# Six reorderings in a two-layer attention and retention block: the modulation tiles in halves, keys and decays, output weights' room, the feed-forward middle block, the first retention head's queries, the second feed-forward's first weights

## The chip, the cores and the metric

The kernel runs on one core of one Trainium2 chip. The metric is the device time of one execution in microseconds (us), from the runs of the kernel; a profile of one execution shows what each engine did. Engines are named as the profile names them: PE (TensorE matmuls), PEld (TensorE weight loads), DVE (VectorE), ACT (ScalarE), POOL (GpSimd), SP (the queue that issues most transfers).

## What is computed

Two layers work on 512 latent tokens and 256 context tokens of width 1024. Layer 0 mixes tokens by windowed grouped-query attention, layer 1 by retention that runs in both directions; each is followed by a SwiGLU feed-forward. All of it is modulated by shifts, scales and gates made from a condition vector ("ada").

```python
for i in range(2):
    mx = split(silu(c) @ ada_w[i] + ada_b[i], 6)          # latent: shift, scale, gate, twice
    mc = split(silu(c_ctx) @ ada_w[i] + ada_b[i], 6)      # context
    h_x = rms_norm(x, norm1_g[i]) * (1 + mx[1]) + mx[0]
    h_c = rms_norm(y_ctx, norm1_g[i]) * (1 + mc[1]) + mc[0]
    if i == 0:    # 16 query heads, 4 key/value heads of 64, q and k normed, 2-D rotary on the latent side,
                  # window of 128 to each side plus all context keys, a sink logit per head
        out_c, out_x = windowed_gqa_sink(h_x, h_c, ...)
    else:         # 4 heads, 256 wide in q and k, 512 wide in v; log decays = log_sigmoid(decay_logit)
        out_c, out_x = bidir_retention(h_x, h_c, ...)     # out = (silu(gate) * norm(o)) @ w_o
    x = x + mx[2] * out_x
    x = x + mx[5] * swiglu(rms_norm(x, norm2_g[i]) * (1 + mx[4]) + mx[3], ffn_w_in[i], ffn_w_out[i])
    # layer 0 does the same for y_ctx with mc
```

The data are fp32.

## The kernel before, in words

**Products.** Matrices are kept transposed, width on the 128 partitions and tokens along the free axis. A float32 product is made of three fp32r matmuls on split operands: a raw weight tile `wraw` (128x1024, one transfer of 512 KB) is cast on ACT to `whi`, and DVE subtracts to get `wlo` (`split`, L165/L166; `next_w`, L140/L141; `split_chunk`, L1321/L1322); activations are split the same way. `mm3` (L148 to L150), `product` (L997), `product_q` (L1391) and `product_v` (L1404) issue hi x hi, hi x lo, lo x hi. Many blocks use a Strassen-like scheme on quarters of a matrix ("seven", seven products instead of eight), with sums of quarters formed on DVE.

**Stages**, by the profile's time: a prologue (0 to 76 us) with the sums of squares, the modulation columns ("ada quarters") and keys and values; queries and attention (76 to 315); the output projection (to about 365); the first feed-forward (to about 860) for latent and context; retention, four heads one after the other (to about 1390); the second feed-forward.

**Order.** Up to the first values of the context a block under `tc.manual_schedule` keeps PE, DVE and ACT in the order in which the code is written. After it a scheduler of the framework orders the instructions of each engine; `after(ins, others)` adds an edge, and the rooms (a tile of a pool is free when its last reader is done) add others. `steps[n]` is a table of functions to be called at step n of attention.

**What the change touches.**

- `ada_quarter_load`, `quarter_product` (L335), `quarter_columns` (L343, L344), `first_quarter` (L353, L357) and `ada_quarter` (L373, L377): quarter q of the modulation is 32 small matmuls on four tiles `adan`, a copy of the resulting rows (ACT, 128x256), two transposes on PE, and some small DVE operations that give the columns. In quarter 0 the scale half is done first; in quarters 1 to 3 both halves go together.
- `hidden0` (L465, L468, L472) makes the modulated hidden tiles `h`, hi and lo, for two of the eight width tiles k; `keys(s, q)` (L481) and `values(s, q)` (L495) use them, s = 0 for latent, 1 for context.
- `rope_key`, `key_factor`, `key_parts` and the loop ahead of them norm, rotate and split the keys; the block `dec` to `dcol` makes the decays of layer 1 from 8 numbers per partition.
- `next_w(wo_p)` takes the four raw tiles of the attention's output weights, `wsel` chooses the room of a raw tile; `w01` is the first feed-forward weight, which waits for `scaled`.
- `seven` of the first feed-forward (L1130 to L1157), 20 times, and `last_sum` (L318, L1058, L1079), which makes the last sums of tokens.
- In a retention head the queries `qt` get their last sums at L1546 and L1549, `rope_pair` rotates them (L1413 to L1415), and sums of the gate and value weights are made at L1564, L1565 and L1571, then split at L1321/L1322 for `product_v`.
- `seven` of the second feed-forward (L1827 on), whose weights b32 and b14 are split at L165/L166.

## Time and profile before

| | |
|---|---|
| runs | 1735.02 us median of 3 (1733.53 to 1737.07) |
| the profiled execution | 1735.58 us, its span 1733.8 us |
| mean granted TensorE clock | 0.999 |
| PE busy | 1705.7 us, 98% of the span, 11092 matmuls |
| DVE busy | 1331.9 us, 77% |
| ACT busy | 843.9 us, 49% |
| DMA | 205.67 MB, mean 119 GB/s |

The span runs from the first to the last instruction that the profile shows; the execution's own time is 1.8 us longer. Matmuls are pipelined, so one that lasts 0.39 us in the table is followed by the next after 0.23 us, and a gap of PE is read from the bracket behind a row: the idle time just before it, and what ended it. Times in the stages are counted from the span's start.

### The profile page before, as it was taken

To read this page: it belongs to the slowest core of one execution; us is meant where nothing else is said; L and a number is where in the kernel's file an instruction comes from. 1 tells how busy PE (TensorE), PEld (TensorE's weight loads), DVE (VectorE), ACT (ScalarE), POOL (GpSimd) and SP (SyncE) were. 2 spreads that over 40 slices of the span, in tenths; PEclk is the share of its full clock that TensorE was granted. 3 is DMA by queue.
4 is the path that set the end of the run, shared out by engine and by line. 5 is a ranking of instruction groups with operands and counts; after the bars stand their busy time and mean duration, and the time that the engine had idled before them with its cause. 6 is when DMAs were issued, how large, how long until landed. Compare 5 with 4: busy or idle time off the path is not lost.

```text
span 1733.8 us, 28152 instructions
## 1 busy us (share of the span) xinstructions
PE 1705.7 (98%) x11092; PEld 1536.9 (89%) x11092; DVE 1331.9 (77%) x2370; ACT 843.9 (49%) x1506; POOL 121.9 (7%) x266
## 2 busy tenths in 40 slices
PE   7999999999999999999999999999999999999999
PEld 5878887899999999999998888898898999999998
DVE  5887796388778787877898858758768898778774
ACT  5667786264434343342564634524525555445442
POOL 0033443000000000000000000000000100000000
PEclk9999999999999999999999999999999999999999
DMA  9510015142234434343423533433433223233322
GB/s 374 201 50 25 14 47 174 49 146 98 98 134 135 138 120 155 110 146 115 141 99 122 176 103 126 158 110 124 158 107 112 98 98 122 74 122 100 107 75 85
DMA packets 61908, 205.67 MB, mean 119 GB/s; under 512 B 6864, under 2 KB 7760, under 8 KB 61648
## 3 DMA queue, kind: packets, MB, share of 16 engines
q1 hardware_dynamic: 54864, 178.71, 29.9%
q0 software_dynamic: 6912, 25.17, 4.4%
q8 instruction: 87, 1.43, 0.3%
q14 instruction: 45, 0.37, 0.1%
HBM read 201.75 MB, written 2.10 MB: 118 GB/s over the span
## 4 chain that ended last, share of the span: by engine, by line
PE 88%; DVE 6%; ACT 3%; DMA 2%; issue 1%; POOL 0%; SPq 0%; DVEq 0%; ACTq 0%
PE Y L997 15%; PE Z L1404 8%; PE Z L997 7%; PE pj L148 6%; PE pj L150 6%; PE pj L149 6%; PE Y L1391 3%; PE X L997 3%; PE pj L1404 3%; PE pO L813 2%; PE pT L788 2%; PE S L768 2%; PE X L1391 2%; PE Z L150 1%; PE Z L149 1%; PE Z L148 1%
## 5 line engine op out<-in xcount | busy, mean ns | idle before, releaser
L165 ACT CAST whi<-wraw 128x1024 fp32r<-128x1024 f32 x98 | 102.4, 1051 | 185.1 <-PE Z L150 75.1
L997 PE MATMUL Y<-aq,whi 128*128 128x384 f32 x640 | 173.7, 335 | 2.4 <-ACT whi L165 1.3
L254 DVE SCALAR_TENSOR_TENSOR res<-pj,mod,res 128x512 f32<-128x512 f32 (+1 forms) x102 | 74.4, 730 | 76.7 <-PE pj L150 75.7
L166 DVE TENSOR_TENSOR wlo<-wraw,whi 128x1024 fp32r<-128x1024 f32 x98 | 119.4, 1223 | 8.9 <-ACT whi L165 8.5
L997 PEld LDWEIGHTS Y<-aq,whi 128*128 128x128 f32 x640 | 116.5, 188 | 3.8 <-ACT hn L1145 1.6
L140 ACT CAST whi<-wraw 128x1024 fp32r<-128x1024 f32 x75 | 78.5, 1048 | 74.5 <-PE Z L150 25.6
L141 DVE TENSOR_TENSOR wlo<-wraw,whi 128x1024 fp32r<-128x1024 f32 x75 | 91.5, 1221 | 25.3 <-ACT whi L140 24.7
L997 PE MATMUL Y<-aq,wlo 128*128 128x384 f32 x320 | 107.0, 334 | 0.0
L272 DVE CUSTOM_DVE_ANT_0 y<-adaw,crow,small_sb 128x1024 bf16<-128x1024 f32 x64 | 81.9, 1279 | 29.3 <-DMA adaw<-in_adaT_dram 29.2
L1321 ACT CAST whi<-wraw 128x1024 fp32r<-128x1024 f32 x55 | 57.6, 1050 | 71.8 <-PE Y L150 52.6
L1404 PE MATMUL Z<-whi,sA 128*128 128x512 f32 x256 | 81.7, 395 | 3.0 <-ACT whi L1321 3.0
L101 ACT ACTIVATE pr<-pr,stat,qs 128x513 f32<-128x513 f32 (+2 forms) x96 | 74.0, 774 | 16.9 <-DVE stat L775 15.1
L1322 DVE TENSOR_TENSOR wlo<-wraw,whi 128x1024 fp32r<-128x1024 f32 x55 | 66.9, 1222 | 17.1 <-ACT whi L1321 17.0
L782 POOL TENSOR_SCALAR pr<-pr,stat 128x512 f32<-128x512 f32 (+2 forms) x96 | 65.1, 693 | 84.5 <-DVE stat L779 78.1
L148 PE MATMUL pj<-ax,whi 128*128 128x512 f32 x176 | 68.9, 391 | 1.3 <-DVE res L254 1.3
L150 PE MATMUL pj<-ax,whi 128*128 128x512 f32 x176 | 68.7, 390 | 0.0
L149 PE MATMUL pj<-ax,wlo 128*128 128x512 f32 x176 | 68.5, 389 | 0.0
L269 POOL DMA_DIRECT2D adaw<-in_adaT_dram x48 | 25.6, 533 | 513.4 <-DVE mod L272 420.9
L769 DVE CUSTOM_DVE_ANT_0 pr<-S,mask,qs 128x256 f32<-128x256 f32 (+1 forms) x96 | 52.7, 567 | 10.8 <-PE S L768 7.2
L997 PE MATMUL Y<-sA,whi 128*128 128x256 f32 x304 | 60.5, 282 | 0.1
L1404 PEld LDWEIGHTS Z<-whi,sA 128*128 128x128 f32 x256 | 48.5, 190 | 13.2 <-ACT whi L1321 3.5
L997 PEld LDWEIGHTS Y<-aq,wlo 128*128 128x128 f32 x320 | 60.1, 188 | 0.0
(615 smaller groups left out, 5479.9 us busy)
## 6 DMA issues: line engine op xcount, KB each, us to landing
wraw<-in_wst_dram SPq DMA_DIRECT2D x231, 512.0 KB, 3.6
adaw<-in_adaT_dram POOLq DMA_DIRECT2D x48, 512.0 KB, 3.7
wx<-in_wst_dram SPq DMA_DIRECT2D x28, 512.0 KB, 4.4
adan<-in_adaQ_dram SPq DMA_DIRECT2D x16, 512.0 KB, 7.0
adan<-in_adaN_dram SPq DMA_DIRECT2D x16, 512.0 KB, 7.4
res<-in_xT_dram SPq DMA_DIRECT2D x16, 256.0 KB, 5.3
q<-in_adaN_dram SPq DMA_DIRECT2D x16, 256.0 KB, 3.2
aq<-in_adaN_dram SPq DMA_DIRECT2D x12, 256.0 KB, 5.3
```

Source lines behind the costliest of these rows:

```text
L140: after(nc.scalar.copy(hi, raw), behind)
L141: after(nc.vector.tensor_tensor(lo, raw, hi, op=sub), low)
L148: after(nc.tensor.matmul(o, whi, xhi, start=first, stop=False), behind)
L149: nc.tensor.matmul(o, wlo, xhi, start=False, stop=False)
L150: return nc.tensor.matmul(o, whi, xlo, start=False, stop=last)
L165: nc.scalar.copy(hi, t)
L166: return nc.vector.tensor_tensor(lo, t, hi, op=sub)
L254: return nc.vector.scalar_tensor_tensor(res[d], o, mods[l, s][:, part, d:d + 1], res[d], mult, add)
L272: after(nc.vector.tensor_tensor_reduce(junk, w, cr[:, s * 1024:(s + 1) * 1024], 1.0, sm_t[:, C_ADAB + l * 48 + j:C_ADAB + l * 48 + j + 1], ...
L997: ins = nc.tensor.matmul(o, p, r, start=first and k + i == 0, stop=k == 3 and i == 2, skip_group_check=not first)
L1391: ins = nc.tensor.matmul(o[:, e * SC:(e + 1) * SC], p[:, ws], r, start=first and k + e + i == 0, stop=k == 3 and i == 2, skip_group_check= ...
L1404: ins = nc.tensor.matmul(o, p, r, start=first and k + i == 0, stop=k == 3 and i == 2, skip_group_check=not first)
```

## The change

It alters the order and the rooms of existing work in six places; the matmuls that carry the arithmetic stay.

1. **Quarters.** `first_quarter` goes, and every quarter is done as quarter 0 was: the scale half (product, copy, transpose, columns), then the shift half. One block of values stands as fill behind each half's copy. The tiles come in the order 2, 3, 0, 1 in each quarter. The matmul that added the last square is replaced by one more DVE addition. `hidden0` issues its multiplications ahead of its ACT operations. The latent `keys` go width tile by width tile.
2. **Keys and decays.** The latent keys' norm and rotation stand earlier; the decays become a function that step 13 of attention calls, behind the scores of block 6.
3. **Output weights' room.** The four raw tiles are taken with `wsel` 2, 3, 4, 5 instead of 0, 2, 3, 1, with four parts of their own in `wo_p`; `w01` waits for nothing but its room.
4. **First feed-forward.** `last_sum` is called in the middle of the first `seven`, behind the split of b24. In every `seven` the cast of the third weight b3 stands behind the copy of the first product.
5. **First retention head.** The queries are rotated between the splits of the two third weights, no longer ahead of the gate and value weights; the rooms of `gate` change.
6. **Second feed-forward.** b14 is split ahead of b32; the casts wait for the last finished block, the subtractions for other additions of the output before.

```diff
     def ada_quarter_load(q):
-        for i in (2, 3, 0, 1) if q == 0 else range(4):
+        for i in (2, 3, 0, 1):
...
+    def ada_quarter(q, w, copy, scale_fill, shift_fill, middle=None):
         o, t = pT()[:, 0:256], pT()[:, 0:256]
+        scales, shifts = (T(st_p, P, "rows", 2) for _ in range(2))
+        quarter_product(o, w, 1)
+        copy(scales, o[:, P:])
+        scale_fill()
+        nc.tensor.transpose(t[:, P:], scales, ident)
+        quarter_columns(q, t, 0, (1,))
+        if middle:
+            middle()
+        quarter_product(o, w, 0)
         nc.scalar.copy(shifts, o[:, 0:P])
+        shift_fill()
+        nc.tensor.transpose(t[:, 0:P], shifts, ident)
+        return lambda: quarter_columns(q, t, 0, (0,)), lambda: quarter_columns(q, t, 1)
-    def ada_quarter(q, w, fill):
-        o = pT()[:, 0:256]
-        for part in range(2):
-            quarter_product(o, w, part, range(4))
-        rows = t_sq(256)
-        nc.scalar.copy(rows, o)
-        fill()
-        t = pT()[:, 0:256]
-        for part in range(2):
-            nc.tensor.transpose(t[:, part * P:(part + 1) * P], rows[:, part * P:(part + 1) * P], ident)
-        quarter_columns(q, t, 0)
-        return lambda: quarter_columns(q, t, 1)
...
     def keys(s, q):
-        steps = [(j, a, b) for j in range(2) for a, b in ((0, 0), (1, 0), (0, 1))]
+        two = (2 * q, 2 * q + 1)
         if s == 0:
-            steps = [steps[i] for i in (0, 1, 3, 4, 2, 5)]
+            steps = [(j, a, 0, k) for k in two for a in range(2) for j in range(2)]
+            steps += [(j, 0, 1, k) for k in two for j in range(2)]
...
-        values(0, 0, (0,))
-        c1 = ada_quarter(1, wq[1], lambda: values(0, 0, (1,)))
+        c0, c1 = ada_quarter(1, wq[1], nc.scalar.copy, lambda: values(0, 0, (0,)), lambda: values(0, 0, (1,)))
...
-        c1 = ada_quarter(3, wq[3], lambda: values(0, 2, (0,)))
+        c0, c1 = ada_quarter(3, wq[3], nc.scalar.copy, lambda: values(0, 2, (0,)), lambda: values(0, 2, (1,)))
+        hidden0(0, 6, 7, shifts=c0, at=1)
         c1()
-        hidden0(0, 6, 7)
-        values(0, 2, (1, 2, 3))
+        values(0, 2, (2, 3))
...
+    def decays(behind):
...
+    steps.setdefault(13, []).append(lambda: decays([blocks[6].scored]))
...
-    for wsel[0] in (0, 2, 3, 1):
-        wo.append(cut(next_w(wo_p)))
+    for wsel[0] in (2, 3, 4, 5):
+        wo.append(cut(next_w(wo_p, 4)))
...
-    def seven():
+    def seven(middle=None):
...
         half = split(g, *b24)
+        if middle:
+            middle()
         nc.vector.tensor_tensor(u[:, l_], u[:, r_], u[:, l_], op=sub)
         b3 = w_parts(fp, 1)
-        split(u, *b3)
+        third = nc.scalar.copy(b3[0], u)
+        nc.vector.tensor_tensor(b3[1], u, b3[0], op=sub)
...
         product(Y, operand["11"], b11, 0, True)
-        after(rounded[0], [nc.scalar.copy(c11, Y)])
+        ins = [nc.scalar.copy(c11, Y)]
+        after(rounded[0], ins)
+        after(third, ins)
...
-    w01 = [next_w(fp, 1, behind=[scaled])]
+    w01 = [next_w(fp, 1)]
...
-                if f == PLAIN:
-                    last_sum()
-                a, end = seven()
+                a, end = seven(last_sum if f == PLAIN else None)
...
-        qh = rope_pair(qt, cos1, sin1)
         if hd:
+            qh = rope_pair(qt, cos1, sin1)
             other_values()
...
-        w3 = [split_chunk(g) for g in g12]
+        w3 = [split_chunk(g12[0])]
+        if not hd:
+            qh = rope_pair(qt, cos1, sin1)
+        w3.append(split_chunk(g12[1]))
...
-            gate[2:4], vt[2:4] = vt[2:4], gate[2:4]
+            gate, vt[2:4] = vt[2:4] + gate[0:2], gate[2:4]
...
-        after(split(u, *b32), added[0:1])
-        after(split(g, *b14), added[1:2])
+        for (hi, lo), t, i in ((b14, g, 1), (b32, u, 2)):
+            after(nc.scalar.copy(hi, t), finished[-1:] if added else [])
+            after(nc.vector.tensor_tensor(lo, t, hi, op=sub), added[i:i + 1])
```

What the engines then do is shown at three places. The first is PE in the prologue, at quarter 1 (the 32 small matmuls `pT<-adan,ccol`, and the transposes from `const_sb`, the identity). Before:

```order
L495 MATMUL kvv<-wlo,h 128x256
L495 MATMUL kvv<-whi,h 128x256
L335 MATMUL pT<-adan,ccol 32x128 x32
L495 MATMUL kvv<-whi,h 128x256
L495 MATMUL kvv<-wlo,h 128x256
L495 MATMUL kvv<-whi,h 128x256 x2
L495 MATMUL kvv<-wlo,h 128x256
L495 MATMUL kvv<-whi,h 128x256
L377 MATMUL pT<-const_sb,sq 128x128 x2
```

Now:

```order
L335 MATMUL pT<-adan,ccol 32x128 x16
L482 MATMUL kvv<-whi,h 128x256
L482 MATMUL kvv<-wlo,h 128x256
L482 MATMUL kvv<-whi,h 128x256 x2
L482 MATMUL kvv<-wlo,h 128x256
L482 MATMUL kvv<-whi,h 128x256
L355 MATMUL pT<-const_sb,rows 128x128
L335 MATMUL pT<-adan,ccol 32x128 x16
L482 MATMUL kvv<-whi,h 128x256
L482 MATMUL kvv<-wlo,h 128x256
L482 MATMUL kvv<-whi,h 128x256 x2
...
L362 MATMUL pT<-const_sb,rows 128x128
```

The 32 small matmuls now come in two groups of 16, with a block of values and a transpose behind each; the block that stood ahead of them stands between them.

The second place is DVE at the first `seven` of the first feed-forward. `wraw<-wraw` of 128x512 are the sums of weight quarters, the row at L1133 (now L1125) the last sum that the split of b24 waits for; `crow<-act` and the `aq` behind it are the last sums of tokens. Before:

```order
L1132 TENSOR_TENSOR wraw<-wraw 128x512
L166 TENSOR_TENSOR aq<-act,aq 128x384 x8
L1058 TENSOR_TENSOR crow<-act 128x384 x3
L1079 TENSOR_TENSOR act<-hn,act 128x384
L1058 TENSOR_TENSOR crow<-act 128x384
...
L166 TENSOR_TENSOR aq<-crow,aq 128x384 x2
L1079 TENSOR_TENSOR act<-hn,act 128x384
L166 TENSOR_TENSOR aq<-crow,aq 128x384 x2
L1133 TENSOR_TENSOR wraw<-wraw 128x512
L166 TENSOR_TENSOR wlo<-wraw,whi 128x1024
```

Now:

```order
L1124 TENSOR_TENSOR wraw<-wraw 128x512
L166 TENSOR_TENSOR aq<-act,aq 128x384 x2
L1125 TENSOR_TENSOR wraw<-wraw 128x512
L166 TENSOR_TENSOR aq<-act,aq 128x384 x2
L166 TENSOR_TENSOR wlo<-wraw,whi 128x1024
L1068 TENSOR_TENSOR hn<-hn,Y 128x384
L166 TENSOR_TENSOR aq<-act,aq 128x384 x8
L1050 TENSOR_TENSOR crow<-act 128x384 x3
...
L166 TENSOR_TENSOR aq<-crow,aq 128x384 x2
L1133 TENSOR_TENSOR wlo<-wraw,whi 128x1024
```

The last weight sum and the low part behind it have moved ahead of the sums of tokens.

The third place is DVE in the first retention head. `wx<-wx` (L1565, now L1560) is the sum for the second weight of the product on values, `gate` the queries' last sums, `hn` and `sq` the rotation (L1413 to L1415, now L1408 to L1410), `wlo<-wx,whi` the low part of a split. Before:

```order
L1322 TENSOR_TENSOR wlo<-wx,whi 128x1024
L1549 TENSOR_TENSOR gate<-gate,Y 128x256 x2
L1413 TENSOR_TENSOR hn<-gate,rj 128x512
L1414 TENSOR_TENSOR sq<-gate,rj 128x512
L1413 TENSOR_TENSOR hn<-gate,rj 128x512
L1415 TENSOR_TENSOR hn<-hn,sq 128x512
L1414 TENSOR_TENSOR sq<-gate,rj 128x512
L1565 TENSOR_TENSOR wx<-wx 128x1024
L166 TENSOR_TENSOR qk<-hn,qk 128x512
L1415 TENSOR_TENSOR hn<-hn,sq 128x512
L1322 TENSOR_TENSOR wlo<-wx,whi 128x1024 x2
```

Now:

```order
L1317 TENSOR_TENSOR wlo<-wx,whi 128x1024
L1544 TENSOR_TENSOR gate<-gate,Y 128x256 x2
L1560 TENSOR_TENSOR wx<-wx 128x1024
L1408 TENSOR_TENSOR hn<-gate,rj 128x512
L1409 TENSOR_TENSOR sq<-gate,rj 128x512
L1317 TENSOR_TENSOR wlo<-wx,whi 128x1024
L1410 TENSOR_TENSOR hn<-hn,sq 128x512
L1317 TENSOR_TENSOR wlo<-wx,whi 128x1024
L1408 TENSOR_TENSOR hn<-gate,rj 128x512
```

The sum for the second weight stands ahead of all six rows of the rotation's arithmetic, where five of them stood ahead of it, and two low parts stand among the first four.

PE takes that second weight earlier too (the numbers tell tiles apart; the second weight is `whi_10182` before and `whi_10175` now). Before, twelve matmuls on the first weight stand ahead of it:

```order
L1404 MATMUL Z_9652<-wlo_10171,sA_9545 128x512
L1404 MATMUL Z_9652<-whi_10170,sA_9546 128x512
L1404 MATMUL Z_9651<-whi_10182,sA_9549 128x512
L1404 MATMUL Z_9652<-whi_10182,sA_9549 128x512
L1404 MATMUL Z_9651<-wlo_10183,sA_9549 128x512
```

Now six:

```order
L1399 MATMUL Z_9662<-wlo_10164,sA_9556 128x512
L1399 MATMUL Z_9662<-whi_10163,sA_9557 128x512
L1399 MATMUL Z_9662<-whi_10175,sA_9560 128x512
L1399 MATMUL Z_9663<-whi_10163,sA_9552 128x512
L1399 MATMUL Z_9663<-wlo_10164,sA_9552 128x512
L1399 MATMUL Z_9663<-whi_10163,sA_9553 128x512
L1399 MATMUL Z_9662<-wlo_10176,sA_9560 128x512
```

Three matmuls of the first weight now stand between the high and the low part of the second.

236 lines of the change are left out of this document (114 added, 122 removed).

## The prediction

> **What bounds the kernel now.** I read the page first, then the waits of PE, then the timeline around each wait. In the page, PE's busy time and its share of the span:
>
> ```profile
> PE 1705.7 (98%) x11092; PEld 1536.9 (89%) x11092; DVE 1331.9 (77%) x2370; ACT 843.9 (49%) x1506; POOL 121.9 (7%) x266
> ```
>
> PE is the bound, and the change leaves its arithmetic as it is. So it can move only the 1733.8 - 1705.7 = 28 us in which PE stands still, and what little PE loses beside its waits. The waits of PE are named in the next view (what waited, for whom, us in total, times, longest):
>
> ```profile
> PE kvv L450 <- DMA res<-in_xT_dram: 4.5, 1, 4.5
> PE pj L481 <- ACT h L468: 3.5, 6, 1.2
> PE Z L1404 <- ACT whi L1321: 3.0, 1, 3.0
> PE pj L697 <- ACT sq L672: 1.5, 2, 1.1
> PE Y L997 <- ACT whi L165: 1.3, 1, 1.3
> ...
> PE pj L148 <- DVE res L254: 1.3, 2, 0.7
> PE pj L148 <- DVE qs L700: 1.2, 1, 1.2
> PE Y L997 <- ACT hn L1145: 1.1, 1, 1.1
> PE S L768 <- DVE q L687: 1.0, 1, 1.0
> PE pT L788 <- ACT tt L794: 0.9, 1, 0.9
> ...
> PE X L148 <- ACT aq L1030: 0.4, 1, 0.4
> ```
>
> The first row is the first load, which no edit touches. The others lie where the edits are: keys (L481), queries (L697, L700, L687), the output weights (L1030), the first feed-forward (L165, L1145), the first retention head (L1404), the second feed-forward (L254). Without the first row they are 15.2 us. The question for each is what is late next.
>
> **The retention head, the largest term.** The timeline around it (start, duration, engine, line; in brackets the idle time before and what ended it), then the windows, with two earlier stretches (us; PE, PEld, DVE, ACT, POOL busy; the granted clock; DMA):
>
> ```profile
> 930.84 1.22 DVE L1322 TENSOR_TENSOR wlo<-wx,whi 128x1024 fp32r<-128x1024 f32 x1
> ...
> 931.97 0.74 DVE L1549 TENSOR_TENSOR gate<-gate,Y 128x256 f32<-128x256 f32 x2
> ...
> 932.06 0.39 PE L1404 MATMUL Z<-whi,sA 128*128 128x512 f32 x1
> ...
> 932.63 0.69 DVE L1413 TENSOR_TENSOR hn<-gate,rj 128x512 f32<-128x512 f32 x1
> ...
> 935.65 1.22 DVE L1565 TENSOR_TENSOR wx<-wx 128x1024 f32<-128x1024 f32 x1
> ...
> 936.89 1.99 ACT L1321 CAST whi<-wx 128x1024 fp32r<-128x1024 f32 x2 [1.12 <-DVE wx L1565]
> ...
> 937.99 1.22 PE L1404 MATMUL Z<-whi,sA 128*128 128x512 f32 x2 [3.04 <-ACT whi L1321]
> ```
>
> ```profile
> 76.00:125.00 49.00, 44.82 (x285) 39.84 (x284) 45.45 (x116) 35.03 (x72) 10.34 (x21) 1.00 0.13 44
> 125.00:315.00 190.00, 188.09 (x1486) 154.23 (x1485) 138.84 (x457) 132.57 (x319) 73.90 (x172) 1.00 0.17 59
> ...
> 935.00:938.00 3.00, 0.01 (x1) 0.01 (x1) 3.00 (x6) 1.72 (x3) 0.00 (x0) 0.99 0.00 0
> 938.00:940.00 2.00, 1.96 (x4) 1.15 (x5) 2.00 (x3) 1.41 (x2) 0.00 (x0) 0.50 0.00 0
> 940.00:942.00 2.00, 2.00 (x8) 1.57 (x7) 2.00 (x4) 0.94 (x2) 0.00 (x0) 0.66 0.00 0
> ```
>
> PE waits 3.04 us for the second weight's high part. Its sum (L1565) stands on DVE behind five rows of the rotation: (935.65 - 932.63) / 5 = 0.60 us each. And the wait costs more than itself: behind it the granted clock is 0.50 for 2 us and 0.66 for 2 us, which loses 1.0 + 0.7 = 1.7 us. This place costs 3.0 + 1.7 = 4.7 us.
>
> Now the sum stands ahead of the rotation: 932.63 + 1.13 (a row of 1024, 931.97 - 930.84) = 933.8, its cast (1.99 / 2 = 1.0) ends at 934.8, its low part, behind a rotation row in flight, at about 936.1. PE asks for the high part after six matmuls now, not twelve: 932.06 + 6 x 0.23 = 933.4, so it waits 1.4 us; four matmuls later, at 935.7, it waits 0.4 us for the low part. The residue is 1.8 to 2.0 us. If that leaves the clock alone, 4.7 - 1.9 = **2.8 us** are won. What is late next is the third and fourth weights, since the rotation now stands among their low parts on DVE; bounds 1.0 (they take back 1.8) and 4.7 (nothing is left).
>
> On the clock the trace shows one case each way: half speed behind 3.04 us of idling, 1.00 from 76 to 125 us, where PE waits up to 1.2 us at a time. The Trainium skill, "TensorE: Matmul & The Clock Gate", Part 1, "What's actually happening", has the clock halve after an idle window of about 3.4 us and come back after as long a busy one; by it a residue of 2 us leaves the clock alone, and 2.8 us stands. This trace agrees in kind, with 3.04 us before and about 3.5 us of slow matmuls behind; where between 1.2 and 3.04 us the point lies no row shows. If the residue halved it all the same, the gain would be 4.7 - 1.9 - 1.7 = 1.1 us.
>
> **First feed-forward.** Two places, both around `seven`:
>
> ```profile
> 408.00 0.69 DVE L1133 TENSOR_TENSOR wraw<-wraw 128x512 f32<-128x512 f32 x1
> 408.73 1.04 ACT L165 CAST whi<-wraw 128x1024 fp32r<-128x1024 f32 x1 [1.95 <-DVE wraw L1133]
> 409.82 0.44 PE L997 MATMUL Y<-aq,whi 128*128 128x384 f32 x1 [1.29 <-ACT whi L165]
> ```
>
> ```profile
> 758.44 1.03 ACT L165 CAST whi<-wraw 128x1024 fp32r<-128x1024 f32 x1
> 759.38 0.48 ACT L1145 COPY hn<-Y 128x384 f32<-128x384 f32 x1
> 759.91 0.45 PE L997 MATMUL Y<-aq,whi 128*128 128x384 f32 x1 [1.11 <-ACT hn L1145]
> ```
>
> At 409.82 the last weight sum L1133 came behind all sums of tokens on DVE; it now stands ahead of most of them, so its cast has long ended when PE asks: **1.3 us** won (bounds 0.8, if the token sums are then late themselves, and 1.5 with the slow first matmul). At 759.91 PE waits for the first product's copy, which stood behind b3's cast of 1.03 us on ACT. Copy first: **0.8 us** (bounds 0, where DVE's delay ahead of it decides, and 1.3).
>
> **Prologue.** One of the three latent key blocks after a quarter, the chip's transfers there, and the next modulation unit:
>
> ```profile
> 28.89 0.49 PE L481 MATMUL pj<-h,whi 128*128 128x512 f32 x1 [0.76 <-ACT h L468]
> 29.56 0.50 PE L481 MATMUL pj<-h,whi 128*128 128x512 f32 x1 [0.17 <-ACT h L468]
> ```
>
> ```profile
> GB/s 0 211 267 330 330 412 420 419 394 414 421 421 399 403 404 423 408 406 413 426 398 411 399 423 418 419 419 407 421 421 414 410 386 396 400 419 309 44 0 0
> ```
>
> ```profile
> 48.88 1.95 PE L308 MATMUL pT<-adan,ccol 128*32 128x128 f32 x64
> ```
>
> Each block waits for the first width tile, runs one matmul, and starts again 0.67 us later instead of 0.23 for the second tile. With four matmuls per tile the second wait is covered: 3 x 0.44 = 1.3 us. The halves bring the first tile 0.8 to 1 us earlier per quarter as well, by my walk along DVE and ACT. But transfers run at 400 to 420 GB/s without a pause to about 66 us (the row is 40 slices of 70 us), and the unit at 48.88 needs tiles that land no earlier than before: PE gets ahead of them and then waits. So **1.2 us** counts (bounds 0 and 2.5). The three extra copies are ACT's, which has room, and the added DVE rows are of 2 to 4 elements.
>
> **Keys, queries, decays.** DVE's row for most of the decays:
>
> ```profile
> 64.91 1.77 DVE L865 SCALAR_TENSOR_TENSOR lg_t<-lg_t,lg_t 128x8 f32<-128x8 f32 x9
> ```
>
> In the window from 76 to 125 us above DVE is busy 45.45 of 49 us, and PE stands still 49 - 44.82 = 4.2 us, in the waits at L697, L700, L687 and L794. Every row taken from DVE and ACT ahead of this stretch lets it start earlier. The decays are 9 such rows in 1.77 us and a dozen others, some 4 us; with the keys' rotation earlier too, I count **1.8 us** (0: the queries' own chain is what is late; 4.2: all of it). They return at step 13, in the next window: DVE is busy 138.84 of 190 us there, PE stands still 1.9 us. I charge **0.5 us** (0 to 2).
>
> **Output weights, second feed-forward.** At the output projection's end a cast waits for a transfer, and PE for it and for the ACT operations behind it:
>
> ```profile
> 362.69 1.05 ACT L140 CAST whi<-wraw 128x1024 fp32r<-128x1024 f32 x1 [1.65 <-DMA wraw<-in_wst_dram]
> ```
>
> With other rooms that transfer is issued earlier, and casts and low parts of two weights leave the stretch: **0.8 us** (0 to 1.6; the 0.4 us at L1030 and smaller ones). In the second feed-forward two waits on L254, 1.3 us in all, come from additions behind low parts on DVE; the low parts now stand further back: **0.6 us** (0 to 1.4).
>
> **The sum**: 2.8 + 1.3 + 0.8 + 1.2 + 1.8 - 0.5 + 0.8 + 0.6 = 8.8 us. The profiled execution took 1735.58 us, so it would take 1726.8; it lies 0.56 us above the median, so 1735.02 - 8.8 = **1726.2 us**.
>
> **Rivals.**
>
> *What is late next takes the small gains.* The prologue is set by transfers, the queries by DVE's own rows, the two feed-forward places by DVE: only retention (2.8), the token sums (1.3) and about 1 us elsewhere stay, 5.1 us: 1729.9. For it speaks DVE's 45.45 of 49 us; against it, that each wait has another releaser. Chance 0.2.
>
> *No change.* The halved clock returns in retention (1.1), attention pays the 2 us bound for the decays, and 1.3 us for the token sums and 1 us elsewhere stay: 1.1 - 2 + 1.3 + 1 = 1.4 us won, 1733.6. Within 0.2% (3.5 us), about what a measurement of this kernel tells from no change. Chance 0.12.
>
> *Slower: b3 in all twenty blocks.* The order change inside `seven` acts in each block, not only in the one that waits:
>
> ```profile
> L1133 DVE TENSOR_TENSOR wraw<-wraw x20: 681/692/694, 408.0 to 832.2; 128x512 f32<-128x512 f32 x20
> ```
>
> ```profile
> 619.09 1.05 ACT L165 CAST whi<-wraw 128x1024 fp32r<-128x1024 f32 x1 [5.75 <-PE Z L150]
> 621.13 0.48 ACT L1145 COPY hn<-Y 128x384 f32<-128x384 f32 x1 [0.99 <-PE Y L997]
> ...
> 627.17 0.33 PE L997 MATMUL Y<-aq,whi 128*128 128x384 f32 x1
> ```
>
> In a usual block the cast ran at 619.09, ahead of the copy; now it follows it, at about 621.6, and with the low part the pair is ready at about 624, some 2.5 us later than before. PE first uses it at 627.17, so 3 us remain and nothing is lost. But the raw tile is free 2.5 us later too, and the next transfer with it. If more than those 3 us are eaten in every block, say by 1 us, the other 19 blocks lose 19 us: 1726 + 19 = 1745. Against it: in the view of waits L997 waits for a cast and for a copy once each in the whole kernel. Chance 0.08.
>
> **How the numbers follow.** The forecast (4.5 to 13 us won) has 0.55, *late next* 0.2, *no change* 0.12, *slower* 0.08, and 0.05 is for the terms' upper bounds together (14 us and more). Low end: 1735.0 - 14.5 = 1720.5; high end takes in *no change* up to 1735. Faster by over 0.2% are the forecast, *late next* and the upper bounds, 0.80; within it 0.12; slower 0.08.
>
> **What would show it.** Right: the wait of L1404's line down from 3.04 to under 2 us and the clock 1.00 throughout 925 to 945; no wait at the first `seven`; L481's waits at 2.2 us or less; PE's idle time about 20 us. Wrong: PE waiting for b3 or a raw tile in many blocks of the first feed-forward, a clock of 0.5 anywhere, or attention's PE idle time above 4 us.

## The result and the profile after

| | before | changed |
|---|---|---|
| runs | 1734.48 us median of 19 (1732.06 to 1737.48) | 1730.35 us median of 19 (1729.10 to 1734.56) |
| ratio, 95% interval | | 0.9979 [0.9972, 0.9985] |
| profiled execution, its span | 1735.58, 1733.8 us | 1730.06, 1728.3 us |

It is faster by 4.1 us between the medians, 0.21% (0.15 to 0.28%) by the ratio, so the interval excludes a ratio of 1, though its lower end lies under the 0.2% that the prediction took for the limit of a measurement. It is inside the range and less than half of the 8.8 us forecast. The page's row of engines, and then the waits of PE in the changed kernel (us in total, times, longest):

```profile
PE 1706.5 (99%) x11090; PEld 1535.7 (89%) x11090; DVE 1336.0 (77%) x2377; ACT 841.4 (49%) x1509; POOL 120.9 (7%) x266
```

```profile
PE kvv L434 <- DMA res<-in_xT_dram: 4.1, 1, 4.1
PE S L756 <- DVE stat L757: 2.8, 2, 2.2
PE kvv L543 <- DVE y L211: 1.8, 1, 1.8
PE pj L468 <- ACT h L453: 1.6, 2, 1.0
...
PE Z L1399 <- ACT whi L1316: 0.6, 1, 0.6
PE Z L1399 <- DVE wlo L1317: 0.6, 1, 0.6
PE pj L148 <- DVE res L1209: 0.6, 1, 0.6
PE pj L685 <- ACT sq L660: 0.5, 1, 0.5
PE Y L989 <- DVE wlo L166: 0.4, 1, 0.4
```

PE stands still 1728.3 - 1706.5 = 21.8 us instead of 28. The waits of before are gone or shorter: the keys (L481, now L468) 1.6 instead of 3.5, retention (L1404, now L1399) 0.6 and 0.6 instead of 3.0, the queries (L697, now L685) 0.5 instead of 1.5, the first `seven` no longer for its cast. But new ones stand in the list: attention's scores for DVE (L756), 2.2 us at once; L1209; a low part (L989 for L166); and, in the prologue, the sum of squares for the DVE addition that replaced a matmul (L543), 1.8 us where it had been 1.3 for ACT (L523).

To see in which stage time comes and goes, I worked out a lead from the two traces: each matmul is counted at the pace of its shape (0.227 us for 128x512, 0.173 for 128x384, 0.118 for 128x256, 0.109 for 128x128), and the lead at a time t is by how much PE had done the same work earlier than in the profile of before. Here it stands beside the terms of the sum:

| stage (time in before) | forecast | lead won |
|---|---|---|
| prologue, to 60 us | +1.2 | +0.9 |
| keys, queries, 60 to 160 | +1.8 | +4.5 |
| decays, 160 to 200 | -0.5 | **-3.2** |
| output weights, first `seven`, 200 to 440 | +0.8 and +1.3 | +1.5 |
| b3 in the first feed-forward, 440 to 920 | +0.8 | **-2.0** |
| retention, 920 to 1020 | +2.8 | +3.0 (4.6, then -1.6) |
| the rest | +0.6 | +0.4 |
| sum | 8.8 | 5.1 |

Two terms are wrong by 2.7 and 2.8 us, and they alone are more than the shortfall, 3.7 us in these two profiles and 4.7 between the medians. The keys brought 2.7 more than thought.

### The profile page after: what moved, and what is told of

Read it like the earlier page. It is cut to its first block, busy times and chain, and to the rows that moved or that the text cites. A ratio compares the mean times of both kernels' runs of the same rounds, so it can differ in the third digit from the quotient of the medians.

```text
span 1728.3 us, 28150 instructions
## 1 busy us (share of the span) xinstructions
PE 1706.5 (99%) x11090; PEld 1535.7 (89%) x11090; DVE 1336.0 (77%) x2377; ACT 841.4 (49%) x1509; POOL 120.9 (7%) x266
## 4 chain that ended last, share of the span: by engine, by line
PE 40%; DVE 7%; DMA 2%; ACT 1%; issue 1%; SPq 0%; ACTq 0%; DVEq 0%
PE Y L989 6%; PE Z L1399 6%; PE Y L1386 3%; PE Z L989 3%; PE pj L148 2%; PE pj L150 2%; PE pj L149 2%; PE pj L1399 2%; PE X L1386 1%; PE X L989 1%; DMA wraw<-in_wst_dram 1%; DVE wlo L1317 1%; PE X L1399 1%; PE X L148 1%; PE X L150 1%
## 5 line engine op out<-in xcount | busy, mean ns | idle before, releaser
L989 PE MATMUL Y<-aq,whi 128*128 128x384 f32 x640 | 173.7, 335 | 1.1 <-ACT hn L1140 0.7
L254 DVE SCALAR_TENSOR_TENSOR res<-pj,mod,res 128x512 f32<-128x512 f32 (+1 forms) x102 | 74.5, 731 | 68.7 <-PE pj L150 68.3
L989 PEld LDWEIGHTS Y<-aq,whi 128*128 128x128 f32 x640 | 116.6, 188 | 2.1 <-ACT hn L1140 1.4
L140 ACT CAST whi<-wraw 128x1024 fp32r<-128x1024 f32 x75 | 78.7, 1049 | 72.1 <-DMA wraw<-in_wst_dram 25.2
L141 DVE TENSOR_TENSOR wlo<-wraw,whi 128x1024 fp32r<-128x1024 f32 x75 | 91.7, 1223 | 28.5 <-ACT whi L140 27.7
L989 PE MATMUL Y<-aq,wlo 128*128 128x384 f32 x320 | 107.2, 335 | 0.5 <-DVE wlo L166 0.4
L272 DVE CUSTOM_DVE_ANT_0 y<-adaw,crow,small_sb 128x1024 bf16<-128x1024 f32 x64 | 81.9, 1280 | 23.1 <-DMA adaw<-in_adaT_dram 23.1
L1316 ACT CAST whi<-wraw 128x1024 fp32r<-128x1024 f32 x55 | 57.6, 1049 | 72.3 <-PE Y L150 52.3
L1399 PE MATMUL Z<-whi,sA 128*128 128x512 f32 x256 | 80.7, 391 | 0.6 <-ACT whi L1316 0.6
L1317 DVE TENSOR_TENSOR wlo<-wraw,whi 128x1024 fp32r<-128x1024 f32 x55 | 67.0, 1223 | 16.4 <-ACT whi L1316 16.3
L165 ACT CAST whi<-wraw 128x1024 fp32r<-128x1024 f32 x40 | 42.0, 1051 | 73.8 <-PE Z L150 43.3
L989 PEld LDWEIGHTS Y<-aq,wlo 128*128 128x128 f32 x320 | 60.1, 188 | 1.1 <-DVE wlo L166 1.1
L757 DVE CUSTOM_DVE_ANT_0 pr<-S,mask,qs 128x256 f32<-128x256 f32 (+1 forms) x96 | 52.7, 567 | 10.7 <-PE S L756 8.5
L148 PE MATMUL pj<-act,whi 128*128 128x512 f32 (+1 forms) x156 | 60.1, 385 | 0.6 <-DVE res L1209 0.6
L989 PE MATMUL Y<-sA,whi 128*128 128x256 f32 x304 | 60.1, 280 | 0.2 <-ACT res L1842 0.2
L1835 ACT CAST whi<-wraw 128x1024 fp32r<-128x1024 f32 x38 | 39.2, 1052 | 43.1 <-DVE wraw L999 21.6
```

What stands on the lines that cost most here:

```text
L140: after(nc.scalar.copy(hi, raw), behind)
L141: after(nc.vector.tensor_tensor(lo, raw, hi, op=sub), low)
L148: after(nc.tensor.matmul(o, whi, xhi, start=first, stop=False), behind)
L254: return nc.vector.scalar_tensor_tensor(res[d], o, mods[l, s][:, part, d:d + 1], res[d], mult, add)
L272: after(nc.vector.tensor_tensor_reduce(junk, w, cr[:, s * 1024:(s + 1) * 1024], 1.0, sm_t[:, C_ADAB + l * 48 + j:C_ADAB + l * 48 + j + 1], ...
L989: ins = nc.tensor.matmul(o, p, r, start=first and k + i == 0, stop=k == 3 and i == 2, skip_group_check=not first)
```

## The experiments

Behind the time of each experiment stand its lowest and highest run and its ratio to the kernel before in the same session, with the 95% interval. The lead at the same times in the profiles of all the kernels (us ahead of the profile of before; the last kernel is before itself, so its row shows how far one run differs from another):

| kernel | 60 | 120 | 160 | 200 | 340 | 440 | 640 | 880 | 920 | 960 | 1020 | 1700 |
|---|---|---|---|---|---|---|---|---|---|---|---|---|
| changed | 0.9 | 4.8 | 5.4 | 2.2 | 2.0 | 3.7 | 3.7 | 1.8 | 1.7 | 6.3 | 4.7 | 5.1 |
| e1 | 0.8 | 4.6 | 5.1 | 5.1 | 5.3 | 6.8 | 6.8 | 4.9 | 4.8 | 8.7 | 6.8 | 7.1 |
| e2 | 0.5 | 4.4 | 4.9 | 4.9 | -3.2 | -1.6 | -1.6 | -3.4 | -3.5 | 1.7 | -0.2 | -0.9 |
| e3 | 0.6 | -1.3 | -1.3 | -1.3 | -1.6 | -1.6 | -1.6 | -0.5 | -0.5 | 3.8 | 1.9 | 1.9 |
| e4 | 0.0 | 3.8 | 4.3 | 1.0 | 0.9 | 2.2 | 2.2 | 1.8 | 1.8 | 7.0 | 4.7 | 3.7 |
| e5 | 1.1 | 4.9 | 5.4 | 5.5 | 5.6 | 6.8 | 6.8 | 7.2 | 7.2 | 11.6 | 9.9 | 9.4 |
| e6 | 1.0 | 4.8 | 4.5 | 4.6 | 4.7 | 6.5 | 6.5 | 4.3 | 4.2 | 7.9 | 6.7 | 5.8 |
| e7 | 1.6 | -1.6 | -1.6 | -2.0 | -2.0 | 0.0 | 0.0 | -0.7 | -0.7 | 3.5 | 1.4 | 0.7 |
| e8 | 1.2 | 5.1 | 5.7 | 5.7 | 5.7 | 5.0 | 5.0 | 5.5 | 5.5 | 9.7 | 7.2 | 7.3 |
| e9 | 1.2 | 5.0 | 5.6 | 5.6 | 5.5 | 6.7 | 6.7 | 6.4 | 6.4 | 10.7 | 9.0 | 9.0 |
| e10 | 1.1 | 4.9 | 5.4 | 5.5 | 5.5 | 6.7 | 6.7 | 8.4 | 8.4 | 12.6 | 10.8 | 10.4 |
| e11 | 0.6 | 0.5 | 0.5 | 0.5 | 0.6 | 0.5 | 0.5 | 1.4 | 1.4 | 3.2 | 3.0 | 2.5 |

So two executions of one kernel differ by 0.6 us at the start, by 0.9 more between 640 and 880, and by 3.0 at 1020; a difference of less than about 1 us in a stretch can't be read from one profile.

### The decays: e1, e2, e6

In the changed kernel the lead goes at one place. The windows there (us; PE, PEld, DVE, ACT, POOL busy; granted clock; DMA), then PE's rows and DVE's (in brackets the idle time before and what ended it):

```profile
164.00:168.00 4.00, 2.75 (x14) 2.27 (x14) 3.87 (x11) 3.00 (x10) 1.74 (x2) 0.90 0.41 131
168.00:172.00 4.00, 4.00 (x22) 3.51 (x21) 3.78 (x18) 1.57 (x4) 0.30 (x2) 0.67 0.01 2
```

```profile
161.96 1.04 PE L776 MATMUL pT<-const_sb,pr 128*128 128x128 f32 x8
165.25 0.45 PE L756 MATMUL S<-k,q 128*128 128x384 f32 x1 [2.25 <-DVE stat L757]
```

```profile
162.02 1.21 DVE L141 TENSOR_TENSOR wlo<-wraw,whi 128x1024 fp32r<-128x1024 f32 x1
163.27 0.68 DVE L675 TENSOR_TENSOR q<-hn,q 64x512 fp32r<-64x512 f32 x1
163.98 0.69 DVE L676 TENSOR_TENSOR q<-hn,q 64x512 fp32r<-64x512 f32 x1
164.70 0.48 DVE L757 CUSTOM_DVE_ANT_0 pr<-S,mask,qs 128x256 f32<-128x256 f32 x1
```

PE's next matmul is a score `S<-k,q`. Its bank (the room in which its sums lie) is free when DVE's reduction at 164.70 has read it; that one stands behind a weight's low part and two splits. PE waits 2.25 us, and the clock falls to 0.90 and 0.67 for the windows behind (0.4 + 1.3 = 1.7 us). The decays' own rows are not in this list: on DVE they ran from 149.6 to 156.3. Is it their time on DVE, as the prediction charged it, or the order that the scheduler makes with them at step 13? Three kernels move only the call.

e1, at once behind the function's definition:

```diff
+    decays([last_key])
...
-    steps.setdefault(13, []).append(lambda: decays([blocks[6].scored]))
```

> The changed kernel with the decays made where they were before, right behind the last key, and all else as changed. Theory D (the decays at step 13 of attention, some 4 us of small rows on DVE, cause the new 2.25 us wait of PE for the scores' bank near 165 us): no PE wait over 1 us between 150 and 180 us, 2 to 3.4 us won there, and 1 to 2 us given back between 76 and 125 us, so 0.5 to 2 us faster than the changed kernel. Rival O (the order of attention changed because the keys are normed earlier; the decays only fall into the same stretch): the wait near 165 us stays at 2 us or more and the kernel is 1 to 2 us slower than the changed one.

1727.96 us (1726.30 to 1730.99), 0.9955 [0.9942, 0.9969]. The lead of 5.1 us is kept through 200, and that of the keys' stretch (4.6 at 120) is there with the decays ahead of it: taking the decays out of that stretch had won nothing. By the ratios it is some 4 us faster than the changed kernel, where 0.5 to 2 had been expected, since nothing was given back between 76 and 125 us.

e2, at step 30, behind the scores of block 15:

```diff
-    steps.setdefault(13, []).append(lambda: decays([blocks[6].scored]))
+    steps.setdefault(30, []).append(lambda: decays([blocks[15].scored]))
```

> The changed kernel with the decays made at step 30 of attention, behind the scores of block 15, instead of step 13. Theory D: the wait near 165 us goes, DVE has more room at step 30, and the lead of 5 us at 160 us is kept to 200 us: 2 to 3.4 us faster than the changed kernel at 315 us; of that some is lost again in the first feed-forward if its lead is bounded by transfers. Rival O: the wait near 165 us stays. Rival M (any place in attention costs as much): a wait of 2 us or more appears near step 30 instead, and the time is that of the changed kernel.

1734.47 us (1729.64 to 1735.91), 0.9990 [0.9981, 0.9999]: it is 2 us slower than the changed kernel by the ratios, not faster. No wait at 165, but two others, for DVE at 231.7 and for a transfer at 270.2, with the clock halved behind the latter (waits of PE, then windows of e2):

```profile
PE pT L911 <- DMA q<-in_adaN_dram: 2.6, 1, 2.6
...
PE pT L776 <- DVE tt L782: 1.2, 1, 1.2
```

```profile
272.00:276.00 4.00, 4.00 (x25) 1.40 (x27) 0.71 (x4) 0.16 (x1) 0.00 (x0) 0.50 0.48 158
276.00:280.00 4.00, 4.00 (x21) 2.06 (x18) 1.86 (x5) 1.93 (x5) 0.00 (x0) 0.67 0.40 111
```

The loss has moved along with the step: 8.1 us of lead are gone by 340, of which the two waits are 3.9 and 6.8 us at half clock 3.4. The transfer that PE waits for was issued at 264.0, where the changed kernel issued it at 261.6; how the step delays it was not followed.

e6, at step 12, one step before the change's place:

```diff
-    steps.setdefault(13, []).append(lambda: decays([blocks[6].scored]))
+    steps.setdefault(12, []).append(lambda: decays([blocks[6].scored]))
```

> The changed kernel with the decays at step 12 of attention, one step earlier, behind the same scores. PE's order then is row for row that with the decays behind the last key, while DVE does the same 4 us of small rows in nearly the same place as in the changed kernel. Theory S (the loss near 165 us comes from PE's order: a row for the scores' bank stands ahead of the queries' rows, and the wait then halves the clock): no wait over 1 us near 165 us, clock 1.00 from 150 to 190 us, lead 4.5 to 5.3 us at 200 us, time within 1 us of the run with the decays at the start. Rival L (DVE's load): a wait of 1.5 us or more between 145 and 175 us, and a lead of 3.5 us or less at 200 us.

1728.47 us (1726.76 to 1729.30), 0.9957 [0.9945, 0.9969], as e1. DVE still does the decays in attention (a group of seven at 146.61; the lead falls by 0.3 us up to 160), but what follows is undisturbed; windows and PE's rows of e6 at the same place, then DVE's rows, of the decays and of the reduction that the score waits for:

```profile
164.00:168.00 4.00, 3.63 (x19) 3.14 (x20) 3.84 (x13) 3.77 (x12) 0.00 (x0) 1.00 0.43 131
168.00:172.00 4.00, 4.00 (x28) 3.58 (x28) 3.99 (x18) 2.31 (x5) 1.60 (x3) 1.00 0.00 2
```

```profile
163.18 0.71 PE L776 MATMUL pT<-const_sb,pr 128*128 128x128 f32 x5
164.37 0.61 PE L685 MATMUL pj<-const_sb,sq 128*128 128x2 f32 x4 [0.48 <-ACT sq L660]
```

```profile
146.61 1.72 DVE L863 SCALAR_TENSOR_TENSOR lg_t<-lg_t,lg_t 128x8 f32<-128x8 f32 x7
...
166.36 0.48 DVE L757 CUSTOM_DVE_ANT_0 pr<-S,mask,qs 128x256 f32<-128x256 f32 x1
```

DVE is as busy as in the changed kernel (3.84 of 4 us against 3.87), its reduction comes even later (166.36 against 164.70), and PE does not wait for it. What differs is the order on PE. In the changed kernel:

```
L776 MATMUL pT<-const_sb,pr 128x128 x8
L756 MATMUL S_2273<-k,q 128x384
L685 MATMUL pj<-const_sb,sq 128x2 x2
L756 MATMUL S_2273<-k,q 128x384
L148 MATMUL pj<-h,whi 128x512
```

and in e6, whose PE has e1's order row for row in attention:

```
L776 MATMUL pT<-const_sb,pr 128x128 x5
L685 MATMUL pj<-const_sb,sq 128x2 x2
L148 MATMUL pj<-h,whi 128x512
L149 MATMUL pj<-h,wlo 128x512
...
L149 MATMUL pj<-h,wlo 128x512
L756 MATMUL S_2273<-k,q 128x384 x2
```

The score that needs DVE stands eleven query matmuls of 128x512 further back, some 2.5 us of work that covers DVE's queue. So the loss is in the order that step 13 brings about, and not in the decays' 4 us on DVE. That the scheduler would do this could be read from its order before any run; that PE would then wait 2.25 us could not.

### The order of b3: e4, e5

e4 undoes only that part, in the changed kernel:

```diff
-        third = nc.scalar.copy(b3[0], u)
-        nc.vector.tensor_tensor(b3[1], u, b3[0], op=sub)
+        split(u, *b3)
...
-        ins = [nc.scalar.copy(c11, Y)]
-        after(rounded[0], ins)
-        after(third, ins)
+        after(rounded[0], [nc.scalar.copy(c11, Y)])
```

> The changed kernel with b3 split as before in all twenty blocks of the first feed-forward (its cast free to run ahead of the copy of the first product). Theory T (the lead that PE loses near 757 and 851 us is bounded by the transfers of the modulation weights, whatever the order of cast and copy): the lead over the kernel before falls by 1.0 to 1.9 us between 660 and 862 us as in the changed kernel, time within 0.8 us of it. Rival C (the later cast frees raw tiles later and so delays transfers): the lead at 862 us is 3 us or more and the kernel is 1 to 1.5 us faster than the changed one.

1730.60 us (1727.42 to 1731.34), 0.9964 [0.9951, 0.9976], which overlaps the changed kernel's ratio. In the trace the loss of 1.9 us between 640 and 880 has shrunk to 0.4. That is against theory T; but the lead at 862 us is 1.9, not the 3 of rival C. e5 takes e1's edit with it (decays at the start, b3 as before):

> The changed kernel with both costly pieces undone: the decays right behind the last key, and b3 split ahead of the copy. If the two losses are separate: the lead over the kernel before is about 5 us at 200 us, 6.8 us at 640 us and falls by no more than 0.5 us to 862 us, then grows by 4 and loses 2 around 990 us; some 1.6 us faster than the run with the decays alone put back, ratio to the kernel before near 0.9945. Rival (at the larger lead the transfers of the modulation weights decide after all): the lead falls by 1.5 us or more between 640 and 862 us again.

1726.31 us (1725.66 to 1727.36), 0.9947 [0.9935, 0.9959]: 9.2 us under before by the ratio, close to what had been forecast for the change. Against e1 it is 1.7 us by the medians, with overlapping intervals. All the profiles together say it better: between 640 and 880 the five with the new order lose 1.9, 2.0, 1.9, 2.2 and 0.7 us of lead (changed, e1, e2, e6, e7), 1.7 in the mean; the seven with the old one gain 1.1, -0.4, 0.4, 0.5, -0.3, 1.7 and 0.9 (e3, e4, e5, e8 to e11), 0.6 in the mean. By the leads the edit costs some 2.3 us. The times go the same way: with the decays out of the way, 0.9955 and 0.9957 with the new order (e1, e6), 0.9942 to 0.9949 with the old one (e5, e8 to e10). Of the changed kernel's 1.9 us, 0.4 go near 665 us, 0.2 near 756 and 1.4 near 853, where e4 loses 0.5 as well. The last two places in the changed kernel (PE's rows, and at the second DVE's and the transfers):

```profile
755.66 0.44 PE L989 MATMUL Y<-aq,whi 128*128 128x384 f32 x1 [0.71 <-ACT hn L1140]
756.54 0.44 PE L989 MATMUL Y<-aq,wlo 128*128 128x384 f32 x1 [0.44 <-DVE wlo L166]
...
837.40 0.69 DVE L1176 TENSOR_TENSOR aq<-wraw,aq 128x512 fp32r<-128x512 f32 x1 [1.10 <-ACT aq L1175]
839.89 1.28 DVE L272 CUSTOM_DVE_ANT_0 y<-adaw,crow,small_sb 128x1024 bf16<-128x1024 f32 x1 [1.79 <-DMA adaw<-in_adaT_dram]
...
841.10 1.89 DVE L1176 TENSOR_TENSOR aq<-wraw,aq 128x512 fp32r<-128x512 f32 x3
841.48 0.53 POOL L269 DMA_DIRECT2D adaw<-in_adaT_dram  x1 [5.96 <-DVE mod L272]
841.82 0.33 SPq L122 DMA_DIRECT2D wraw<-in_wst_dram  x1
...
848.79 1.28 DVE L272 CUSTOM_DVE_ANT_0 y<-adaw,crow,small_sb 128x1024 bf16<-128x1024 f32 x1 [0.92 <-DMA adaw<-in_adaT_dram]
850.54 0.39 PE L148 MATMUL pj<-act,whi 128*128 128x256 f32 x1 [0.61 <-DVE res L1209]
```

and the same rows of DVE and the same transfers in e4:

```profile
838.04 1.30 DVE L1173 TENSOR_TENSOR aq<-wraw,aq 128x512 fp32r<-128x512 f32 x2 [1.48 <-ACT aq L1172]
...
839.36 0.33 SPq L122 DMA_DIRECT2D wraw<-in_wst_dram  x1
...
841.44 1.28 DVE L272 CUSTOM_DVE_ANT_0 y<-adaw,crow,small_sb 128x1024 bf16<-128x1024 f32 x1 [2.10 <-DMA adaw<-in_adaT_dram]
...
843.03 0.53 POOL L269 DMA_DIRECT2D adaw<-in_adaT_dram  x1 [6.11 <-DVE mod L272]
```

The transfer at 841.82 waits for a raw tile of the output weights, which DVE's rows `aq<-wraw` read last (L1176, in e4 L1173). In the changed kernel DVE takes one of these four rows and then L272, which waits 1.79 us for `adaw`, so the tile is free only behind that; in e4 it takes two ahead of L272. So the weight's transfer starts 0.3 us behind one for `adaw` (512 KB each) and not 3.7 us ahead of it. By the transfers' records both then land at 848.8 to 848.9, 7.1 to 7.3 us after their issue; in e4 they take 4.6 and 4.0 us. DVE's L272 waits 0.92 us for `adaw`, L1209 behind it is late, and PE waits 0.61 us. All five kernels with the new order of b3 have one such row ahead of L272, and 0.3 us between the transfers; the seven with the old one and before have two. So here, too, the edit acts through the order that the scheduler makes around it, now on DVE. The raw tile that b3's own cast reads is released later as well (its next transfer starts at 835.86, in e4 at 833.98), but nothing waits for that transfer here.

And at 756 the wait that the edit was to remove has become 0.71 us for the copy and 0.44 for the low part, 1.15 against 1.11 in the profile of before. That 1.11 is itself of one execution: e11, the same kernel, waits 0.45 us there and e3, with the same order, 0.28.

### The keys: e7

e7 is e1 with the latent keys' norm and rotation where they stood before (the whole reordering of the prologue's last 20 lines, in which the context's keys and two units of the modulation move too; its core):

```diff
-        key_rows(0, kvx[0])
-        key_rows(2, kvx[1])
...
+    key_rows(0, kvx[0])
+    key_rows(1, kvc)
+    key_rows(2, kvx[1])
...
+        rope_key(kn[2])
+        key_last = key_factor(2)
```

> The changed kernel with the decays and the keys' norm and rotation both where they were before; quarters and all else as changed. Theory K (the lead won between 76 and 125 us, 3 to 4 us, comes from the keys' earlier norm and rotation, which takes DVE and ACT rows out of the queries' way): the lead at 125 us falls to 1 to 2 us, waits of about 1 us at the queries' statistics and scores return, and the kernel is 2 to 3.5 us slower than with the decays alone put back. Rival H (the halves of the quarters bring it, by an earlier start of DVE): the lead at 125 us stays at 4 us or more and the time within 0.8 us.

1733.60 us (1731.21 to 1736.03), 0.9989 [0.9980, 0.9997]: 5.6 us above e1, more than theory K's 2 to 3.5. Its lead is 1.6 us at 60 and 80, and -1.6 at 120. In its profile the clock is at half for 6.8 us from 97.2 on, behind these waits, which is 3.4 us of that fall. The four waits of before are back (waits of PE in e7):

```profile
PE pj L685 <- ACT sq L660: 1.5, 2, 1.0
PE pj L148 <- DVE qs L688: 1.2, 1, 1.2
PE S L756 <- DVE q L675: 1.0, 1, 1.0
PE pT L776 <- ACT tt L782: 0.9, 1, 0.9
```

In the changed kernel PE stands still 0.8 us in all from 76 to 125 us, where it had been 4.2:

```profile
76.00:125.00 49.00, 48.18 (x314) 42.07 (x314) 44.17 (x121) 36.30 (x78) 13.03 (x28) 1.00 0.14 44
```

DVE's work there, 44.17 us, is hardly less than the 45.45 of before. The difference lies at the start of the stretch; the changed kernel, then e7:

```profile
76.00:84.00 8.00, 7.49 (x52) 6.81 (x50) 6.71 (x11) 6.87 (x12) 0.00 (x0) 1.00 0.20 66
```

```profile
76.00:84.00 8.00, 6.96 (x48) 6.32 (x47) 7.88 (x14) 7.57 (x13) 0.00 (x0) 1.00 0.00 0
```

DVE is busy 6.71 of 8 us there against 7.88 (7.88 in before, too), and the first split of queries (L675) stands at 86.3 us, against 87.4 in e7 and 89.5 in before. So the keys' earlier place clears DVE and ACT (6.87 against 7.57) where the queries' chain starts, as the prediction had it; which of the two decides is not shown. It won about what the prediction had as its upper bound.

### The first retention head: e3, e11

e3 is before with only the edit of the queries (its hunk in the diff of the change).

> The kernel before with the first retention head's edit alone (queries rotated between the two third weights, rooms of the gate). If the prediction's step was only sized too low: 3.0 to 4.7 us won between 925 and 950 us, no granted clock under 0.95 there, 1.0 to 1.6 us lost again near 990 us where the changed kernel waits 0.63 us for a low part, so 1.5 to 3.5 us faster than before. Rival: the edit in itself is worth 0 to 1 us, and the changed kernel's gain there comes from the other edits' lead.

1734.27 us (1732.93 to 1735.86), 0.9990 [0.9982, 0.9999]: 1.7 us by the ratio. The trace has 4.3 us of lead won at the place and 1.9 given back by 1020. The changed kernel does the same; its rows, and its window over the whole place:

```profile
931.29 0.73 PE L1399 MATMUL Z<-whi,sA 128*128 128x512 f32 x2 [0.64 <-ACT whi L1316]
...
985.32 0.50 PE L1399 MATMUL Z<-wlo,aq 128*128 128x512 f32 x1 [0.63 <-DVE wlo L1317]
```

```profile
925.00:945.00 20.00, 19.30 (x100) 15.83 (x99) 19.73 (x26) 10.35 (x15) 0.00 (x0) 1.00 0.29 94
```

So the residue at 931 is smaller than forecast, and a later low part takes some back. But the comparison with one profile was also flattering. e11 is before once more, in one execution.

> The kernel before, unchanged, profiled once more. Theory W (whether a wait of about 1 us halves the clock depends on where it falls in a running window, so it changes from run to run): the waits at the queries' statistics and scores between 80 and 120 us are the same to 0.2 us, but the granted clock there need not be 1.00 again: below 0.95 in some 4 us between 80 and 120 us has a chance of one half. The wait of 3.0 us near 938 us is followed by half clock again. Rival: the clock follows the waits alone, so it is 1.00 from 80 to 120 us as in the first profile.

1733.04 us. Its rows at the place, and the windows behind:

```profile
935.26 0.73 PE L1404 MATMUL Z<-whi,sA 128*128 128x512 f32 x2 [2.27 <-ACT whi L1321]
936.52 0.50 PE L1404 MATMUL Z<-wlo,sA 128*128 128x512 f32 x1 [0.53 <-DVE wlo L1322]
```

```profile
935.00:938.00 3.00, 2.21 (x8) 1.53 (x9) 3.00 (x4) 2.04 (x4) 0.00 (x0) 1.00 0.00 0
938.00:940.00 2.00, 2.00 (x10) 1.58 (x9) 2.00 (x3) 1.33 (x3) 0.00 (x0) 1.00 0.00 0
```

2.8 us of waiting in place of 3.04, and the clock stays at 1.00. The 1.7 us of slow matmuls, which the prediction counted as part of this place, were there in one execution and not in the other. Against e11 the changed kernel wins 1.4 us from 920 to 1020, not 3.0. The waits between 80 and 120 us left the clock at 1.00 in e11 as well.

### Output weights, last sums, second feed-forward: e8, e9, e10

e9 and e10 are e5 with one edit as before, e8 with three: the rooms of the output weights, `w01` and the order of b32 and b14:

```diff
-    for wsel[0] in (2, 3, 4, 5):
-        wo.append(cut(next_w(wo_p, 4)))
+    for wsel[0] in (0, 2, 3, 1):
+        wo.append(cut(next_w(wo_p)))
...
-    w01 = [next_w(fp, 1)]
+    w01 = [next_w(fp, 1, behind=[scaled])]
...
-        for (hi, lo), t, i in ((b14, g, 1), (b32, u, 2)):
...
+        after(split(u, *b32), added[0:1])
+        after(split(g, *b14), added[1:2])
```

> As the run with both costly pieces undone, but with the rooms of the output weights, the first feed-forward weight's wait and the splits of b14 and b32 as before. By the prediction's terms 0.8 us of lead are missing at 380 us and 0.6 us at 1440 us; by the changed kernel's profile 1.7 us and 0.5 us. So 1.4 to 2.2 us slower than the run with both costly pieces undone. Rival (the leads are lost again behind those places): within 0.6 us of it.

1726.77 us (1725.88 to 1727.76), 0.9949 [0.9937, 0.9961]: 0.5 us from e5, not to be told apart, though it wins 1.9 us less lead from 340 to 440. At the first `seven` PE waits again, with the last sums out of the way:

```profile
401.74 0.44 PE L989 MATMUL Y<-aq,whi 128*128 128x384 f32 x1 [0.74 <-ACT whi L165]
```

e9, b32 and b14 alone (the last part of that diff):

> As the run with both costly pieces undone (decays behind the last key, b3 split ahead of the copy), but with b14 and b32 of the second feed-forward split in the order and with the waits of before. The prediction gave that edit 0.6 us. Theory N (it is worth nothing: the waits on L254 near 1422 us go and a wait for an ACT copy near 1455 us comes): lead at 1700 us within 0.6 us of the run with it, time within 0.8 us of it. Rival (the prediction's term): 0.6 to 1.4 us slower.

1725.03 us (1723.30 to 1726.09), 0.9942 [0.9928, 0.9955]: the new order wins nothing that the times can tell. In e5, which has it, a wait takes the place of the one removed:

```profile
1454.40 0.39 PE L989 MATMUL Y<-sA,whi 128*128 128x256 f32 x1 [1.46 <-ACT res L1839]
```

e10, `last_sum` ahead of the first `seven`:

```diff
-                a, end = seven(last_sum if f == PLAIN else None)
+                if f == PLAIN:
+                    last_sum()
+                a, end = seven()
```

> As the run with both costly pieces undone, but with the last sums of tokens ahead of the first seven again. The prediction gave the move 1.3 us. If that holds, PE waits 1.2 to 1.5 us for the cast of L165 near 402 us, and the lead at 440 us is 1.0 to 1.5 us smaller than with the move. Rival (with the output weights' rooms changed, DVE is early enough, so the wait is gone anyway): the lead at 440 us is within 0.4 us.

1724.64 us (1723.90 to 1726.67), 0.9945 [0.9932, 0.9957]; the lead won from 340 to 440 is e5's (1.2 us). PE's wait at the first `seven` in e10 (0.35 us in e5):

```profile
402.67 0.44 PE L989 MATMUL Y<-aq,wlo 128*128 128x384 f32 x1 [0.60 <-DVE wlo L166]
```

With the new rooms (and `w01` without its wait, which e8 does not separate from them) the last weight sum is no longer late even behind the sums of tokens, so moving them is worth no more than about 0.3 us. e5, e9 and e10 are 9 to 10 us faster than before and, by the ratios, some 5 to 6 us faster than the changed kernel; they cannot be told apart from one another.

## Why the prediction was right in sign and wrong in size

**What held.** PE's idle time fell to 21.8 us ("about 20"), L1399 waits 1.3 us and the clock is 1.00 from 925 to 945, the keys' waits are 1.6 us, the first `seven` doesn't wait for its cast. The waits that the edits were to remove are gone or less than half, except b3's, and one of the two on L254 (0.7 us).

**The decays' charge failed** (-0.5 forecast, -3.2 in the trace; 1.2 beyond the end of its bound). It was priced as DVE's time in a stretch where PE stood still 1.9 of 190 us, and so as nearly free. The step that failed is the assumption behind that price, that a moved step costs only the time of the rows it issues. It also moves its neighbours: the scheduler put a score that needs a late bank ahead of query matmuls that need nothing, PE waited 2.25 us, and the halved clock behind it took 1.7 more. e6, one step earlier with the same rows on DVE, has no such wait.

**The term for b3 failed in sign** (+0.8 forecast, about 2 us lost). The gain was priced from a wait of 1.11 us that two other executions with the same order have at 0.45 and 0.28. The slower rival came near with a late transfer, but not by its path or its price of 1 us in each of 19 blocks: at the largest place, near 853 us, the transfer was late because DVE's rows were put into another order, and it then met another on the second queue. The step that failed is that the 3 us until PE's first use of b3 cover the whole edit. The prediction followed only b3 and the transfer into its raw tile; PE waited for what DVE's new order held up.

**The keys were sized too low** (+1.8 forecast, +3.9 from 60 to 120 and up to 5.6 by e7). The 1.8 was taken between the bounds with the decays as part of the reason; e1 shows that the decays had no part in it.

**Retention, last sums, b14.** The 2.8 rested on the half clock of one execution. The place brought 4.6 us in the trace, of which 1.6 were given back, near the lower bound's 1.8; that it came to 3.0 is partly luck, since the profile of before has the half clock, and against e11 it is 1.4. The last sums' 1.3 and the output weights' 0.8 came to 1.5 together, since the rooms (with `w01`) already cure the wait at the first `seven`. The 0.6 for b14 are not seen in e9.

Together: the decays 2.7 worse, b3 2.8 worse, the smaller terms 0.9 worse, the keys and queries 2.7 better, so 3.7 of the 8.8 are missing. e5, the change without its two losing edits, gave 9.2 us. That the keys' surplus fills what the small terms lacked makes its nearness to the forecast partly luck.

## What to carry to other kernels

Price a moved step by the order that the scheduler makes around it: look in PE's order for matmuls that need another engine's late result and now stand ahead of work that needs nothing, and try the neighbouring step as well, since one step made 2.4 us of lead at 200 us here. Do the same for the other engines: look which last read of a raw tile now stands behind a wait, and follow the next transfer to what it then shares the DMA with, not only to its own reader. And where a term holds a stretch of halved clock, take more than one profile before counting it.
